# The order of the terms in a split matmul stream, factors made a stage sooner, and the decays of a gated linear attention made later

## The chip, the cores and the metric

One core of one Trainium2 chip. The metric is the device time of one execution in microseconds; smaller is better. The kernel was timed in 3 runs.

## What is computed

One layer of a streaming encoder for 512 tokens of width 2048, all in float32. The input projection of the normalised input is cut into nine parts: q, k, v and gate of a stick-breaking attention (8 heads of 128), q, k (512 wide), v and gate of a gated linear attention (4 heads), and a low-rank input of 16 columns for the decays.

```python
h = rms_norm(x, norm_gain[layer])
proj = jnp.einsum('bsd,de->bse', h, w_in[layer])
(sb_q, sb_k, sb_v, sb_g, gl_q, gl_k, gl_v, gl_g, gl_lr) = jnp.split(proj, offsets, axis=-1)
...
a_out = stick_breaking_attention(q, k, v)
a_out = from_heads(rms_norm(a_out, ...)) * jax.nn.silu(sb_g)
gate_logits = jnp.einsum('bsr,rk->bsk', gl_lr, gla_w_alpha[layer]) + gla_b_alpha[layer]
log_alpha = jax.nn.log_sigmoid(gate_logits.astype(jnp.float32)) / GLA_GATE_TAU
b_out = gated_linear_attention(..., log_alpha)
b_out = from_heads(rms_norm(b_out, ...)) * jax.nn.silu(gl_g)
mixed = jnp.concatenate([a_out, b_out], axis=-1)
x = x + jnp.einsum('bse,ed->bsd', mixed, w_out[layer])
```

The linear attention multiplies q by exp(cum) and k by exp(-cum), where cum is the running sum of log_alpha within a chunk: these are the decays of this text.

## The kernel before, in words

**Split products.** The large products run in a reduced float32 format (fp32r). To keep precision, each factor is held as two parts, hi (the rounded value) and lo (the rest), and a product is three terms: ah x hi, ah x lo and al x hi, where ah and al are the parts of the left factor (activations) and hi and lo those of the right one (weights). `split` (L173) makes a weight's parts: hi by a cast on ACT (L177), lo by a subtraction on DVE (L178), 128x1024 each. The parts of a left factor are made in `_split` (ACT L290, DVE L291, 128x512).

**Stages.** The work is ten stages in a row on TensorE (PE). Two are direct: q (tag q) and k (tag k), where `direct` (L293) sums over 4 units u and two parities odd, and for each of the two token halves issues 12 matmuls of 128x512 into two of the four accumulators z. The low-rank columns ride along in stage k (`rank_products`, L641, 4 matmuls after each half). The other eight are pairs (`pair`, L319): two 2048x512 weight blocks are done together by a scheme with 7 half-sized products in place of 8. Its left factors are blocks of the activations (A11, A12, A22) and sums of them: D = A22 - A21, NQ = -(D + A11), S3 = A11 - A21, S4 = D + A11 - A12. A pair goes through four sub-stages: (0, 1) A11 into x and D into y for each unit, (2) NQ into x and S4 into y, (3) A12 into y and S3 into x, then A22 into x; 28 products of 12 matmuls, which `mult` (L328) issues. The pairs are, in order: qv, vk, gqk (with the operands' roles exchanged, 24 matmuls of 128x256 a product), gv, ga, gb (all with the left factor h), then o0 and o1 (the output projection, left factor m, the gated mixture). In the names of tiles, hi_qva, qvp, qvq, qvb, qvc, qvd, qve are a pair's split weights in the order of use (a goes with A11, p with D, q with NQ, b with S4, c with A12, d with S3, e with A22); D_h, S_h, D_m, S_m are left factors, st and pw the weight tiles that `load` (L167) fetches and `add` (L183) sums, with `gather` (L188) adding a block by a DMA that GpSimd (POOL) issues.

**Left factors.** `Acts.get` gives a left factor for one unit. D and S3 are made at first use and kept; A11, A12, A22, NQ and S4 are written to DRAM and loaded again by each later pair. D costs a subtraction on DVE (L227) and a split, S3 the same (L216). h's D and S3 are first used in pair qv, m's in pair o0; m is complete for a group of columns when its two `gate` chains (L952) have run, counted in m_done.

**Order.** PE runs in the order of the program text. Everything that isn't a block product (the attention, the linear attention, the gates, the decays) is written as a generator; `side.step()`, which stands between block products, advances the first chain whose time has come. A chain yields a number, to be left alone for so many microseconds of matmul time as the program counts them, or a condition. The instructions of the other engines are put in order by a scheduler at build time, with a higher priority for what stands under `urgent()`; at run time each engine runs its own list. Side work takes one of four PSUM banks (`ptile`), block products four others: two accumulators x, two y. The next pair's x takes the banks that came free first, its y the last ones.

**Decays** (L667). After `low_rank` the chain waits 6.0, then for each of four heads issues one matmul (lg), copies it with its bias on ACT (lgs, L683, urgent), takes Abs, Exp and Ln on ACT (lge, L685 to L687), on DVE a combination (L688), a scan (L690) and a subtraction (L695), on ACT amid (L693) and two exponentials qe and ke (L697, L698), and on DVE three products with these (L701 to L704); it yields 3.0 between heads. The chain is spawned ahead of pair vk; gqk's results are multiplied by qe and ke, and wait for all four heads. The instructions of pair vk that end it are the evacuations of x_vk into sv_1 (ACT L153, DVE L157), scaled.

Of the kernel before, what the change touches and what calls it, by code (L numbers as in the profile page):

```python
# [13 lines left out]
P = 128  # L14
S = 512
D = 2048
NK = D // P
NB = S // P
KU = 2
NU = NK // KU  # L20
HU = NU // 2
H2 = 2 * P
# [71 lines left out]
def body(ctx: ExitStack, tc: tile.TileContext, x, xT, w_in, w_lr, w_alpha, vecs, w_out, out):  # L94
# [11 lines left out]
    side = Sides()  # L106

    def mm(o, l, r, **kw):
        n = r.free_size()
        side.t += n * (1.75 if l.dtype == F32 else 0.443) * 1e-3  # L110
        nc.tensor.matmul(o, l, r, **kw)  # L111
# [20 lines left out]
    def drop(n):  # L132
        held[0] -= n

    def room(n):
        return lambda: held[0] + n <= NU4
# [156 lines left out]
    def direct(A, s, tag, o, before=None, extra=None, last=False):  # L293

        z = [pacc.tile([P, S], F32, name=f"z_{tag}{j}", tag="acc") for j in range(NB)]
        for u in range(HU):
            for odd in range(2):
                if before is not None:
                    before(odd, u)
                hi, lo = split(load(s[odd * HU + u], f"{tag}{odd}{u}"), f"{tag}{odd}{u}")  # L300
                first, final = u == 0 and odd == 0, u == HU - 1 and odd == 1
                for half in range(2):
                    t = A.block(odd, half, u, last)
                    for a in range(2):
                        js = slice(a * P, (a + 1) * P)
                        for i in range(KU):
                            ah, al = t[:, 0, i, js], t[:, 1, i, js]
                            for n, (l, r) in enumerate(((ah, hi[:, i]), (ah, lo[:, i]), (al, hi[:, i]))):
                                mm(z[2 * half + a], l, r, start=first and i == 0 and n == 0,
                                   stop=final and i == KU - 1 and n == 2, skip_group_check=True)  # L310
                        side.step()
                    if extra is not None:
                        extra(odd, half, u, t)
        for half in range(2):
            o.finish(z[2 * half:2 * half + 2], half, 1.0, None)

# [2 lines left out]
    def pair(A, s1, s2, tag, o1, o2, order=(0, 1, 2, 3), tmajor=True, before=None):  # L319
# [3 lines left out]
        acc = {}  # L323
# [4 lines left out]
        def mult(f, u, w, acc, start, stop):  # L328
            t = A.get(f, u)
            hi, lo = w  # L330
            if tmajor:
                for a in range(2):
                    js = slice(a * P, (a + 1) * P)
                    for i in range(KU):
                        ah, al = t[:, 0, i, js], t[:, 1, i, js]
                        for n, (l, r) in enumerate(((ah, hi[:, i]), (ah, lo[:, i]), (al, hi[:, i]))):
                            mm(acc[a], l, r, start=start and i == 0 and n == 0,
                               stop=stop and i == KU - 1 and n == 2, skip_group_check=True)
                    if a == 0:
                        side.step()  # L340
            else:
                for c in range(4):
                    cs = slice(c * P, (c + 1) * P)
                    o = acc[c // 2][:, (c % 2) * H2:(c % 2 + 1) * H2]
                    for i in range(KU):
                        ah, al = t[:, 0, i], t[:, 1, i]
                        for n, (l, r) in enumerate(((hi[:, i, cs], ah), (hi[:, i, cs], al), (lo[:, i, cs], ah))):
                            mm(o, l, r, start=start and i == 0 and n == 0 and c % 2 == 0,
                               stop=stop and i == KU - 1 and n == 2, skip_group_check=True)
                    if c == 1:  # L350
                        side.step()
            side.step()

        first, last = order[0], order[-1]
# [191 lines left out]
    ps = ptile("warm_ps")  # L546
# [65 lines left out]
    lr = {}  # L612
# [25 lines left out]
        nc.vector.tensor_tensor(wa[64:96, :], wst[0:32, :], wa[0:32, :].bitcast(F32), ALU.subtract)  # L638
        low.append(wl)

    def rank_products(odd, half, u, t):  # L641

        if "ps" not in lr:
            lr["ps"] = ptile("lr_ps")
            lr["n"] = 0
        ts = slice(half * H2, (half + 1) * H2)
        for i in range(KU):
            for hl in range(2):
                lr["n"] += 1
                mm(lr["ps"][:, ts], lr[odd][:, u * KU + i, :], t[:, hl, i], start=lr["n"] == 1, stop=lr["n"] == 4 * NK,  # L650
                   skip_group_check=True)
        if lr["n"] == 4 * NK:
            drop(2)

# [11 lines left out]

    def decays():  # L667
        yield lambda: "lr" in done
        yield 6.0
        yield room(5)  # L670
        wa, lrT = low[0][:, 0, :], low[0][:, 1, :]
        blk = ut("blk")[:, 0, :]
# [5 lines left out]
        for h in range(GH):  # L678
            ps = ptile(f"lg{h}")
# [26 lines left out]
            if h == GH - 1:  # L706
                drop(2)
            if h < GH - 1:
                yield 3.0
        done.add("decays")  # L710


# [237 lines left out]
    me, mo, m_done = {}, {}, [0] * 4  # L950
# [41 lines left out]
    h = Acts("h", lambda u: he[u], lambda u: ho[u], ("D", "S3"))  # L992
# [31 lines left out]
    for hd in range(4):  # L1024
        side.spawn(gla_head(hd, ki, qd, gv, hd == 3))
    pair(h, w_in[6], w_in[7], "ga", gate(0), gate(1))
    pair(h, w_in[12], w_in[13], "gb", gate(2), gate(3))
    drop(8)


# [1 line left out]
        if stage == 0:  # L1032
            side.until(lambda: m_done[u] == 2)

    m = Acts("m", lambda u: me[u], lambda u: mo[u], ("D", "S3"))
    order = (0, 1, 3, 2)
    pair(m, w_out[0], w_out[1], "o0", Residual(0), Residual(1), order=order, before=ready)
    drop(10)
# [45 lines left out]
```

## Time and profile before

| | us |
|---|---|
| runs | 918.75, 916.96, 923.38 |
| median | 918.75 |
| the profiled execution | 924.25 |
| its span on the core | 922.4 |

The profile shows one execution: every instruction of the five engines (PE TensorE, PEld its weight loads, DVE VectorE, ACT ScalarE, POOL GpSimd), what ended an engine's idle time, and the clock that TensorE was granted, as a share of 2.4 GHz (0.50 is the lower of its two levels, 1.2 GHz). Over the whole span the mean granted clock was 0.957. The stages begin at about 8 (q), 64 (k), 116 (qv), 203 (vk), 332 (gqk), 444 (gv), 540 (ga), 642 (gb), 730 (o0) and 834 us (o1).

### The profile page before, as it was taken

The numbers are of one execution on the slowest core, as the hardware profiler recorded it, in microseconds if no ns is written. First come the engines' busy times: TensorE is split into PE (matmuls) and PEld (weight loads), VectorE is DVE, ScalarE is ACT, GpSimd is POOL, SyncE is SP. The second block draws the span as 40 slices with busy tenths as digits, with TensorE's granted clock in tenths as the row PEclk, the third lists the DMA queues.
The fourth block names the chain that finished last, engine by engine and source line by source line (L and its number), as shares of the span: only waits on it lengthen the run. The fifth ranks groups of instructions, "written<-read, shape, count | busy, mean of one in ns | idle before, by whom it ended". The sixth has DMA issues, their size and how long they took to land.

```text
span 922.4 us, 11401 instructions
## 1 busy us (share of the span) xinstructions
PE 841.4 (91%) x4082; PEld 700.2 (76%) x4082; DVE 667.1 (72%) x821; ACT 482.4 (52%) x822; POOL 75.0 (8%) x113
## 2 busy tenths in 40 slices
PE   8889999899779899899799899999998899779988
PEld 5678877678657699899687688878886777658766
DVE  4441699669886897788865676769856999777654
ACT  4464466466775656554564336456644845433331
POOL 1000000101111120220100100100001000000000
PEclk8999999999879899999899999999999999899999
DMA  8878326994447664776348973599579637999894
GB/s 316 285 263 287 134 92 243 322 346 160 160 129 218 199 207 158 241 228 240 132 145 281 316 282 101 174 327 344 195 248 298 238 118 262 291 340 344 277 337 126
DMA packets 62040, 216.97 MB, mean 235 GB/s; under 512 B 7040, under 2 KB 7168, under 8 KB 61984
## 3 DMA queue, kind: packets, MB, share of 16 engines
q1 hardware_dynamic: 54928, 195.26, 58.9%
q0 software_dynamic: 4608, 16.78, 10.1%
q10 hardware_dynamic: 2448, 4.21, 1.2%
q8 instruction: 32, 0.52, 0.2%
q14 instruction: 24, 0.20, 0.1%
HBM read 191.06 MB, written 25.17 MB: 234 GB/s over the span
## 4 chain that ended last, share of the span: by engine, by line
PE 49%; DVE 20%; DMA 17%; issue 8%; ACT 5%; POOL 1%; SPq 0%; DVEq 0%; ACTq 0%; POOLq 0%
PE x_o L111 5%; PE z_k L111 4%; PE x_ga L111 4%; PE x_gb L111 3%; PE x_gv L111 3%; PE y_o L111 3%; PE z_q L111 3%; PE y_gqk L111 3%; PE x_gqk L111 3%; PE y_gb L111 3%; PE y_ga L111 2%; PE x_vk L111 2%; PE y_gv L111 2%; DMA st_o0d<-in_w_out 2%; PE a L111 2%
## 5 line engine op out<-in xcount | busy, mean ns | idle before, releaser
L111 PE MATMUL z_q<-hi_q,A_h 128*128 128x512 f32 x128 | 44.1, 422 | 8.9 <-ACT A_h L290 4.9
L111 PE MATMUL z_k<-hi_k,A_h 128*128 128x512 f32 x128 | 42.3, 391 | 0.0
L111 PEld LDWEIGHTS z_q<-hi_q,A_h 128*128 128x128 f32 x128 | 25.9, 204 | 17.4 <-ACT A_h L290 6.2
L111 PEld LDWEIGHTS z_k<-hi_k,A_h 128*128 128x128 f32 x128 | 24.1, 188 | 4.7
L111 PE MATMUL z_q<-lo_q,A_h 128*128 128x512 f32 x64 | 26.8, 419 | 0.5 <-DVE lo_q L178 0.5
L178 DVE TENSOR_TENSOR lo_k<-st_k,hi_k 128x1024 fp32r<-128x1024 f32 x8 | 9.8, 1224 | 23.6 <-ACT hi_k L177 23.6
L111 PE MATMUL z_k<-lo_k,A_h 128*128 128x512 f32 x64 | 25.1, 392 | 0.0
L188 POOL DMA_DIRECT2D pw_o<-in_w_out x8 | 7.0, 870 | 183.2 <-DVE st_o1d L183 80.0
L178 DVE TENSOR_TENSOR lo_q<-st_q,hi_q 128x1024 fp32r<-128x1024 f32 x8 | 9.7, 1223 | 12.5 <-ACT hi_q L177 12.5
L188 POOL DMA_DIRECT2D pw_qv<-in_w_in x4 | 3.6, 906 | 175.9 <-DVE st_qvd L183 175.9
L111 PE MATMUL x_o<-hi_o0d,S_m 128*128 128x512 f32 x32 | 12.5, 454 | 5.3 <-DVE S_m L291 4.4
L111 PEld LDWEIGHTS z_q<-lo_q,A_h 128*128 128x128 f32 x64 | 13.0, 203 | 3.7 <-DVE lo_q L178 1.0
L111 PE MATMUL x_vk<-hi_vkd,S_h 128*128 128x512 f32 x32 | 12.3, 436 | 3.7 <-ACT hi_vkd L177 3.7
L177 ACT CAST hi_q<-st_q 128x1024 fp32r<-128x1024 f32 x8 | 8.3, 1048 | 11.7 <-PE z_q L111 11.7
L111 PE MATMUL y_o<-hi_o0p,D_m 128*128 128x512 f32 x32 | 11.7, 429 | 2.5 <-ACT D_m L290 1.5
L111 PE MATMUL x_o<-hi_o1d,S_m 128*128 128x512 f32 x32 | 11.8, 432 | 2.3 <-ACT hi_o1d L177 2.3
L943 ACT ACTIVATE ja<-an 128x128 f32<-128x128 f32 x32 | 9.9, 308 | 7.6 <-DVE an L155 7.0
L111 PE MATMUL x_qv<-hi_qvd,S_h 128*128 128x512 f32 x32 | 11.5, 423 | 2.5 <-ACT hi_qvd L177 2.5
L111 PEld LDWEIGHTS z_k<-lo_k,A_h 128*128 128x128 f32 x64 | 12.1, 189 | 1.9
L587 ACT ACTIVATE xt<-xt 128x1024 f32<-128x1024 f32 x8 | 8.5, 1061 | 9.6 <-DMA xt<-in_x 9.6
L111 PE MATMUL y_vk<-hi_vkb,S_h 128*128 128x512 f32 x32 | 13.4, 470 | 0.0
L860 ACT ACTIVATE cs_B<-cs_B 128x512 f32<-128x512 f32 x8 | 5.1, 633 | 16.0 <-POOL cs_B L858 15.8
(644 smaller groups left out, 2970.2 us busy)
## 6 DMA issues: line engine op xcount, KB each, us to landing
A_h<-far_A_h SPq DMA_DIRECT2D x72, 512.0 KB, 5.5
NQ_h<-far_NQ_h SPq DMA_DIRECT2D x20, 512.0 KB, 4.3
S_h<-far_S_h SPq DMA_DIRECT2D x20, 512.0 KB, 3.4
far_A_h<-A_h SPq DMA_DIRECT2D x12, 512.0 KB, 4.0
far_A_m<-A_m SPq DMA_DIRECT2D x12, 512.0 KB, 7.3
A_m<-far_A_m SPq DMA_DIRECT2D x12, 512.0 KB, 7.9
st_q<-in_w_in SPq DMA_DIRECT2D x8, 512.0 KB, 4.5
st_k<-in_w_in SPq DMA_DIRECT2D x8, 512.0 KB, 3.8
```

Of the source, the lines that this page charges most:

```text
L111: nc.tensor.matmul(o, l, r, **kw)
L177: nc.scalar.copy(hi, t)
L178: nc.vector.tensor_tensor(lo, t, hi.bitcast(F32), ALU.subtract)
L188: nc.gpsimd.dma_start(t, src, accum_op=ALU.add)
L587: nc.scalar.activation(xt, xt, AF.Square, accum_out=ss8[:, j * 2 + i:j * 2 + i + 1])
L860: nc.scalar.activation(cs, cs, AF.Exp)
L943: nc.scalar.activation(junk, an[:, tb * P:(tb + 1) * P], AF.Square, accum_out=ss[:, tb:tb + 1])
```

## The change

Four parts. (A) In `direct` and `mult` the terms with hi (8 of a product's 12 matmuls) come first for the whole product and the terms with lo last; `direct` takes both token halves together, 16 matmuls with hi and 8 with lo, and the low-rank matmuls of both halves come behind them. (B) `rank_products` makes D and S3 of h, unit by unit, during stage k. (C) The left factor m is declared ahead of pair gb, and in gb's sub-stages 2 and 3, at the units 1 and 3, D and S3 of m's groups 0 and 1 are made. (D) The decays' first wait is 50.0 instead of 6.0, and that between heads 8.0 instead of 3.0. In `mult` the branch with exchanged roles (gqk) is changed in the same way as the one shown.

```diff
                 first, final = u == 0 and odd == 0, u == HU - 1 and odd == 1
-                for half in range(2):
-                    t = A.block(odd, half, u, last)
-                    for a in range(2):
-                        js = slice(a * P, (a + 1) * P)
+                ts = [A.block(odd, half, u, last) for half in range(2)]
+                for low_part in (False, True):
+                    for j in range(NB):
+                        t, js = ts[j // 2], slice(j % 2 * P, (j % 2 + 1) * P)
                         for i in range(KU):
                             ah, al = t[:, 0, i, js], t[:, 1, i, js]
-                            for n, (l, r) in enumerate(((ah, hi[:, i]), (ah, lo[:, i]), (al, hi[:, i]))):
-                                mm(z[2 * half + a], l, r, start=first and i == 0 and n == 0,
-                                   stop=final and i == KU - 1 and n == 2, skip_group_check=True)
-                        side.step()
-                    if extra is not None:
-                        extra(odd, half, u, t)
+                            if low_part:
+                                mm(z[j], ah, lo[:, i], start=False, stop=final and i == KU - 1, skip_group_check=True)
+                            else:
+                                mm(z[j], ah, hi[:, i], start=first and i == 0, stop=False, skip_group_check=True)
+                                mm(z[j], al, hi[:, i], start=False, stop=False, skip_group_check=True)
+                        if j % 2:
+                            side.step()
+                if extra is not None:
+                    extra(odd, u, ts)
...
             if tmajor:
-                for a in range(2):
-                    js = slice(a * P, (a + 1) * P)
-                    for i in range(KU):
-                        ah, al = t[:, 0, i, js], t[:, 1, i, js]
-                        for n, (l, r) in enumerate(((ah, hi[:, i]), (ah, lo[:, i]), (al, hi[:, i]))):
-                            mm(acc[a], l, r, start=start and i == 0 and n == 0,
-                               stop=stop and i == KU - 1 and n == 2, skip_group_check=True)
-                    if a == 0:
+                for low_part in (False, True):
+                    for a in range(2):
+                        js = slice(a * P, (a + 1) * P)
+                        for i in range(KU):
+                            ah, al = t[:, 0, i, js], t[:, 1, i, js]
+                            if low_part:
+                                mm(acc[a], ah, lo[:, i], start=False, stop=stop and i == KU - 1, skip_group_check=True)
+                            else:
+                                mm(acc[a], ah, hi[:, i], start=start and i == 0, stop=False, skip_group_check=True)
+                                mm(acc[a], al, hi[:, i], start=False, stop=False, skip_group_check=True)
+                    if not low_part:
                         side.step()
...
-    def rank_products(odd, half, u, t):
+    def rank_products(odd, u, blocks):
...
+        if odd:
+            h.get("D", u)
+            h.get("S3", u)
         if lr["n"] == 4 * NK:
...
         yield lambda: "lr" in done
-        yield 6.0
+        yield 50.0
         yield room(5)
...
             if h < GH - 1:
-                yield 3.0
+                yield 8.0
...
-    pair(h, w_in[12], w_in[13], "gb", gate(2), gate(3))
+    m = Acts("m", lambda u: me[u], lambda u: mo[u], ("D", "S3"))
+
+    def ahead(stage, u):
+        if stage >= 2 and u in (1, 3):
+            n = stage - 2
+            side.until(lambda: m_done[n] == 2)
+            side.until(room(3))
+            m.get("D" if u == 1 else "S3", n)
+
+    pair(h, w_in[12], w_in[13], "gb", gate(2), gate(3), before=ahead)
...
-    m = Acts("m", lambda u: me[u], lambda u: mo[u], ("D", "S3"))
```

On PE, the last unit of pair qv's sub-stage 3 (x_qv_920 and 921, after the change 958 and 959, are the two accumulators x; hi_qvd and lo_qvd the split weights, S_h the left factor S3). Before:

```order
L111 MATMUL x_qv_920<-hi_qvd_1478,S_h_1483 128x512
L111 MATMUL x_qv_920<-lo_qvd_1479,S_h_1483 128x512
L111 MATMUL x_qv_920<-hi_qvd_1478,S_h_1483 128x512 x2
L111 MATMUL x_qv_920<-lo_qvd_1479,S_h_1483 128x512
L111 MATMUL x_qv_920<-hi_qvd_1478,S_h_1483 128x512
L111 MATMUL x_qv_921<-hi_qvd_1478,S_h_1483 128x512
```

After:

```order
L111 MATMUL x_qv_958<-hi_qvd_1483,S_h_914 128x512 x4
L111 MATMUL x_qv_959<-hi_qvd_1483,S_h_914 128x512 x4
L111 MATMUL x_qv_958<-lo_qvd_1484,S_h_914 128x512 x2
L111 MATMUL x_qv_959<-lo_qvd_1484,S_h_914 128x512 x2
L111 MATMUL y_qv_960<-hi_qvc_1478,A_h_1503 128x512 x4
L111 MATMUL y_qv_961<-hi_qvc_1478,A_h_1503 128x512 x4
```

The second matmul of a product read lo; now the ninth does, and the last two of each accumulator. Behind them the next product (y_qv) begins with its hi terms.

On ACT, where pair vk ends and gqk begins (sv_1 is the evacuation of x_vk; lgs, lge, amid, qe and ke are steps of the decays; cs_B, an, y_k belong to the attention). Before:

```order
L860 ACTIVATE cs_A_2578<-cs_A_2578 128x512
L177 CAST hi_gqka_2789<-st_gqka_2785 128x1024
L177 CAST hi_gqkp_2832<-pw_gqk_2787 128x1024
L153 ACTIVATE sv_1_2778<-x_vk_1631,rstd 128x512
L177 CAST hi_gqka_2864<-st_gqka_2860 128x1024
L860 ACTIVATE cs_B_2639<-cs_B_2639 128x512
L554 ACTIVATE y_k_2691<-v_k_2688 128x16
```

After:

```order
L702 ACTIVATE lge_2632<-lge_2632 128x512
L701 ACTIVATE lge_2725<-lge_2725 128x512
L151 COPY an_2789<-a_2777 128x512
L702 ACTIVATE lge_2725<-lge_2725 128x512
L875 ACTIVATE cs_B_2601<-cs_B_2601 128x512
L565 ACTIVATE y_k_2678<-v_k_2675 128x16
L708 ACTIVATE amid_2638<-lge_2632 128x4
L566 ACTIVATE y_k_2678<-y_k_2678 128x16
L712 ACTIVATE qe_2371<-lgs_2630 128x512
L713 ACTIVATE ke_2372<-lgs_2630 128x512
L153 ACTIVATE sv_1_2744<-x_vk_1630,rstd 128x512
```

Before, sv_1 came right after two casts of weights; now steps of the decays of two heads stand ahead of it, qe and ke among them.

On DVE, the same place (the other half of sv_1; w_A is the evacuation of the transposes wT_A of PE, lo_gqkp the lo of the weights for gqk's first y product). Before:

```order
L946 TENSOR_TENSOR on_1_2331<-an_2539,r_a_2557 128x2x128
L854 SCALAR_TENSOR_TENSOR cs_B_2639<-runs,e_B_2632 128x512
L178 TENSOR_TENSOR lo_gqkp_2833<-pw_gqk_2787,hi_gqkp_2832 128x1024
L157 TENSOR_SCALAR sv_1_2778<-x_vk_1630,rstd 128x512
L855 TENSOR_TENSOR cs_B_2639<-zB_2624,cs_B_2639 128x512
L808 TENSOR_TENSOR v_k_2688<-ss_k_1627,rstd_104 128x16
```

After:

```order
L178 TENSOR_TENSOR lo_gqkp_2896<-pw_gqk_2862,hi_gqkp_2895 128x1024
L155 COPY w_A_2568<-wT_A_2819 128x512
L183 TENSOR_TENSOR pw_gqk_2753<-pw_gqk_2753,st_gqkb_3123 128x1024
L870 TENSOR_TENSOR cs_B_2601<-zB_2586,cs_B_2601 128x512
L703 SCALAR_TENSOR_TENSOR lgs_2630<-lgs_2630,lge_2632 128x512
L824 TENSOR_SCALAR v_k_2675<-v_k_2675 128x16
L705 SCALAR_TENSOR_TENSOR lge_2632<-blk,lgs_2630 128x512
L703 SCALAR_TENSOR_TENSOR lgs_2723<-lgs_2723,lge_2725 128x512
L710 TENSOR_TENSOR lgs_2630<-lge_2632 128x512
L568 TENSOR_TENSOR t_k_2681<-y_k_2678 128x16
L705 SCALAR_TENSOR_TENSOR lge_2725<-blk,lgs_2723 128x512
L157 TENSOR_SCALAR sv_1_2744<-x_vk_1631,rstd 128x512
```

The evacuation sv_1 followed lo_gqkp; now it stands behind w_A, an addition of weights and the decays' combination, scan and subtraction.

On DVE in pair gb, sub-stage 3 (st_gbd is the weight sum for S3 of h, one per unit; lo_gbc and lo_gbd the lo parts; D_m and dq_m steps of D of m; ge and z steps of the gates). Before:

```order
L183 TENSOR_TENSOR st_gbd_6081<-pw_gb_5726,st_gbd_6081 128x1024
L958 TENSOR_SCALAR z_0_6029<-z_0_6029 128x1024
L178 TENSOR_TENSOR lo_gbc_6084<-st_gbc_6079,hi_gbc_6083 128x1024
L178 TENSOR_TENSOR lo_gbd_6089<-st_gbd_6081,hi_gbd_6088 128x1024
L178 TENSOR_TENSOR lo_gbc_6124<-st_gbc_6119,hi_gbc_6123 128x1024
L965 TENSOR_TENSOR ge_0_6055<-ge_0_6055,z_0_6029 128x1024
L183 TENSOR_TENSOR st_gbd_6121<-pw_gb_5771,st_gbd_6121 128x1024
L969 TENSOR_TENSOR ge_0_6055<-ge_0_6055,on_0_5199 128x1024
L178 TENSOR_TENSOR lo_gbd_6129<-st_gbd_6121,hi_gbd_6128 128x1024
```

After:

```order
L183 TENSOR_TENSOR st_gbd_6095<-pw_gb_5726,st_gbd_6095 128x1024
L291 TENSOR_TENSOR D_m_6089<-dq_m_5909,D_m_6089 128x512
L235 TENSOR_TENSOR dq_m_5909<-dq_m_5909,me_5499 128x512
L183 TENSOR_TENSOR st_gbd_6135<-pw_gb_5771,st_gbd_6135 128x1024
L178 TENSOR_TENSOR lo_gbd_6103<-st_gbd_6095,hi_gbd_6102 128x1024
L980 TENSOR_TENSOR ge_0_6067<-ge_0_6067,z_0_6039 128x1024
L178 TENSOR_TENSOR lo_gbc_6138<-st_gbc_6133,hi_gbc_6137 128x1024
L984 TENSOR_TENSOR ge_0_6067<-ge_0_6067,on_0_5199 128x1024
L178 TENSOR_TENSOR lo_gbd_6143<-st_gbd_6135,hi_gbd_6142 128x1024
```

The lo of the second unit (lo_gbd_6089, after the change lo_gbd_6103) came before the third unit's sum; now it comes behind it and behind two steps of D of m.

## Rows read from the trace of the kernel before

**Rows 1.** The page's first part: busy us, share of the span, instructions.

```profile
PE 841.4 (91%) x4082; PEld 700.2 (76%) x4082; DVE 667.1 (72%) x821; ACT 482.4 (52%) x822; POOL 75.0 (8%) x113
```

**Rows 2.** TensorE's waits: line, released by, us in total, times, longest.

```profile
PE T_q L115 <- ACT lgs L683: 6.9, 1, 6.9
...
PE x_o L111 <- DVE S_m L291: 4.4, 1, 4.4
...
PE x_o L111 <- DVE lo_o0e L178: 4.0, 1, 4.0
...
PE T_k L115 <- ACT lgs L683: 3.6, 1, 3.6
...
PE y_gqk L111 <- DVE lo_gqkb L178: 2.4, 1, 2.4
...
PE wT_C L115 <- DVE cs_A L855: 2.2, 1, 2.2
...
PE y_o L111 <- ACT D_m L290: 1.5, 1, 1.5
...
PE y_o L111 <- DVE D_m L291: 1.0, 1, 1.0
...
PE y_gb L111 <- DVE lo_gbb L178: 0.3, 1, 0.3
```

**Rows 3.** Windows: stretch, length, busy of PE, PEld, DVE, ACT, POOL; clock; DMA share, GB/s.

```profile
64.00:116.00 52.00, 52.00 (x260) 44.13 (x259) 21.08 (x34) 26.13 (x67) 0.00 (x0) 1.00 0.56 193
116.00:203.00 87.00, 80.46 (x345) 64.46 (x345) 74.14 (x91) 49.17 (x90) 4.26 (x6) 0.98 0.73 247
130.00:145.00 15.00, 12.53 (x57) 9.53 (x55) 14.21 (x23) 9.09 (x15) 0.00 (x0) 1.00 0.21 70
160.00:175.00 15.00, 14.39 (x64) 11.58 (x63) 12.47 (x16) 7.45 (x10) 1.88 (x2) 1.00 1.03 336
203.00:332.00 129.00, 110.16 (x516) 91.05 (x515) 105.18 (x136) 86.64 (x184) 24.17 (x34) 0.91 0.60 190
249.80:256.60 6.80, 5.41 (x15) 4.44 (x16) 6.73 (x11) 2.65 (x6) 1.56 (x3) 0.50 0.35 60
263.40:270.30 6.90, 4.69 (x15) 3.79 (x16) 6.80 (x11) 5.31 (x9) 0.92 (x2) 0.51 0.20 76
290.00:332.00 42.00, 35.92 (x172) 29.47 (x171) 34.72 (x48) 24.93 (x61) 11.88 (x14) 0.92 0.70 220
730.00:765.00 35.00, 30.06 (x123) 23.40 (x122) 33.97 (x44) 17.60 (x23) 0.00 (x0) 0.91 0.32 115
792.50:799.30 6.80, 5.08 (x12) 4.02 (x13) 5.74 (x7) 1.94 (x3) 0.86 (x1) 0.50 0.87 253
```

**Rows 4.** The chain that ended last: start us, us, what (pair gb; pair o0).

```profile
655.21 2.72 PE x_gb L111 x12
...
784.12 8.19 DMA st_o0d<-in_w_out
...
792.34 1.23 DVE st_o0d L183
793.56 0.60 DVE S_m L291
```

**Rows 5.** Timeline of DVE: start us, us, line, tiles, idle before and releaser.

```profile
245.31 0.68 DVE L688 SCALAR_TENSOR_TENSOR lgs<-lgs,lge 128x512 f32<-128x512 f32 x1
246.03 1.23 DVE L690 TENSOR_TENSOR_SCAN lge<-blk,lgs 128x512 f32<-128x512 f32 x1
...
330.79 0.74 DVE L157 TENSOR_SCALAR sv<-x_vk,rstd 128x512 f32<-128x512 f32 x1
...
703.34 1.22 DVE L183 TENSOR_TENSOR st_gbd<-pw_gb,st_gbd 128x1024 f32<-128x1024 f32 x1 [2.42 <-DMA st_gbd<-in_w_in]
```

**Rows 6.** Timeline of ACT, decays in vk and the end of vk.

```profile
262.68 0.63 ACT L697 ACTIVATE qe<-lgs 128x512 f32<-128x512 f32 x1 [0.97 <-DVE lgs L695]
...
329.67 0.69 ACT L153 ACTIVATE sv<-x_vk,rstd 128x512 f32<-128x512 f32 x1 [1.67 <-PE x_vk L111]
```

More of the change, by code (lines that the diff above doesn't have):

```diff
@@ L340, in mult @@
                         side.step()
             else:
[L342 to L350, printed above, removed]
+                for low_part in (False, True):
+                    for c in range(4):
+                        cs = slice(c * P, (c + 1) * P)
+                        o = acc[c // 2][:, (c % 2) * H2:(c % 2 + 1) * H2]
+                        for i in range(KU):
+                            ah, al = t[:, 0, i], t[:, 1, i]
+                            if low_part:
+                                mm(o, lo[:, i, cs], ah, start=False, stop=stop and i == KU - 1, skip_group_check=True)
+                            else:
+                                mm(o, hi[:, i, cs], ah, start=start and i == 0 and c % 2 == 0, stop=False,
+                                   skip_group_check=True)
+                                mm(o, hi[:, i, cs], al, start=False, stop=False, skip_group_check=True)
+                    if not low_part:
@@ L645, in rank_products @@
             lr["n"] = 0
[L646 to L651, printed above, removed]
+        for half, t in enumerate(blocks):
+            ts = slice(half * H2, (half + 1) * H2)
+            for i in range(KU):
+                for hl in range(2):
+                    lr["n"] += 1
+                    mm(lr["ps"][:, ts], lr[odd][:, u * KU + i, :], t[:, hl, i], start=lr["n"] == 1,
+                       stop=lr["n"] == 4 * NK, skip_group_check=True)
+        if odd:
+            h.get("D", u)
+            h.get("S3", u)
         if lr["n"] == 4 * NK:
```

## The prediction

> **What bounds the kernel now.** I read the busy time of the engines first, then TensorE's list of waits, then a table of windows by stage, then the chain of waits, and last the timelines of single stretches. The reader is to see in [rows 1] that TensorE (PE) is busy for 841.4 of 922.4 us: the bound is the matmul stream, and all that a change of order can win is the 81 us in which it stands and the time in which it runs at the lower of its two levels. The wait list [rows 2] names who makes it stand: casts and subtractions that split the weights, left factors made too late (D_m, S_m), and two transposes (T_q, T_k) that wait for the PSUM bank which `lgs`, the first step of the decays, has not yet emptied. The windows [rows 3] give the price that follows a stand: after the waits of the decays the granted clock is 0.50 and 0.51 (the 1.2 GHz level) for 6.8 and 6.9 us, after the wait for S_m 0.50 for 6.8 us. Half of the PE time in such a stretch is a loss: (5.41 + 4.69) / 2 = 5.0 us for the first two together. Undisturbed, a product of 12 matmuls takes 2.72 us [rows 4], 0.227 us a matmul.
>
> **A, hi terms first.** The matmuls stay the same in number and shape. Before, the first matmul that reads lo stood one behind the first that reads hi; now eight stand ahead of it (see the order of the pair qv). That is 7 x 0.227 = 1.59 us more for the subtraction on VectorE (DVE), which takes 1.2 us. TensorE's waits for a lo of L178 are 17 rows of the list, the first 4.0 and the last 0.3 us [rows 2], 20.2 us in sum. The two rows over 1.6 us (4.0 and 2.4) keep 2.4 and 0.8; the rest, 17.0 us, could go. That is the upper end. But DVE is what is late there: where it is behind by its own queue, the wait comes back a product later, at hi. The lower end is 0: the left factor's lo is read 0.23 us sooner than before, and the first of two banks is finished two matmuls from the end instead of six, so its evacuation starts 0.9 us later. I take 8, near the middle, as most rows are single waits of under 1.6 us with cover enough and a few are not.
>
> **B, D and S3 of h in the direct k stage.** Per unit: four DVE instructions of 128x512 (0.68 us by [rows 5]) and two casts on ScalarE (ACT). For four units 16 x 0.68 = 11 us of DVE leave pair qv. They issue no DMA, since these factors are kept. In qv, DVE is busy 74.14 of 87.00 us, and in 130 to 145 us 14.21 of 15.00 while PE has 12.53 [rows 3]. In the k stage PE never stands, and DVE is busy for 21.08 of 52.00: it hides the 11 us there. One lo_k can fall back by the 2.7 us of a unit's four; sixteen hi matmuls now stand ahead of its first reader, 15 x 0.227 = 3.4 us, and without that cover each unit would cost up to 2.7. The most that can be won is qv's idle time, 87.00 - 80.46 = 6.5, with the 2% that the clock lacks, 1.7: 8. The least is 0, if the loads end last there. I take 5, nearer the upper end as the engine full in that stretch is the one relieved.
>
> **C, D and S3 of m, groups 0 and 1, inside pair gb.** 8 DVE instructions (5.4 us) and 4 casts leave o0 and its first stretch, where DVE is busy 33.97 of 35.00 us [rows 3]. There y_o waits 1.5 and 1.0 us for D_m, and x_o 4.4 us for S_m [rows 2]; the half clock after the latter costs 5.08 / 2 = 2.5 [rows 3]. The sum, 9.4, and 2.6 for half of the first stretch's missing clock make the upper end, 12; the D_m waits alone, 2.5, make the lower. I take 6: S_m stands behind an addition (`st_o0d`, L183) that waits for a load of 8.19 us [rows 4], so part of it becomes a wait for that load's own split. The price is in gb. The order shows `lo_gbd_6103` (the lo of the second unit of that stage) now behind two D_m steps and behind the third unit's addition `st_gbd_6135`, which waits for its load: before, such an addition waited 2.42 and took 1.22 us [rows 5]. Less A's cover, 2.42 + 1.22 - 1.59 = 2; with D_m's two steps and a half clock 7. I take 2 lost (0 to 7).
>
> **D, the decays later and spread.** Removed from vk: T_q 6.9, T_k 3.6 and wT_C 2.2 [rows 2], with the 5.0 of half clock 17.7 us, the upper end. The lower is T_q with its stretch, 6.9 + 2.3 = 9. I take 14: the attention's own work still fills DVE there (105.18 of 129.00 us, [rows 3]). But the work is moved, not removed: the decays' heads 2 and 3 now fall on the end of vk, where DVE is already busy 34.72 of 42.00 us. The order shows the new wait. At the change from vk to gqk the evacuations of x_vk (`sv_1`) free the banks that y_gqk needs. Before, they came at 329.67 and 330.79 us, right after the last x_vk, and the list has no wait of y_gqk for them [rows 2, 5, 6]. Now the DVE one stands behind `w_A`, which waits for wT_A on PE, and wT_A is the last thing PE does ahead of y_gqk. After wT_A, DVE has to do five steps of 128x512 (0.68), one of 128x1024 (1.22), two scans (1.23) and `sv_1` itself (0.74): 3.4 + 1.2 + 2.5 + 0.7 = 7.8 us [rows 5]. The ACT one stands behind `qe` and `ke` (0.63 each, [rows 6]), which wait for the seventh of those DVE steps: 5.9 + 1.3 + 0.7 = 7.8 as well. PE has nothing to do meanwhile, since its order is fixed. A half clock follows, as after T_q (2.3), and DVE's backlog ahead of `w_A` I put at 1.4: 11.5 lost. The low bound is 3 (7.0 by the overlap of DVE's steps, less 4 that the loads and splits gain while PE stands), the high one 17 (a backlog twice that of one addition and 6.8 us at half clock).
>
> Here the Trainium skill bears on the sum. The page "TensorE: Matmul & The Clock Gate", section "Architectural detail: the array is 16x 32x32, not 1x 128x128", says that ACT and DVE work strictly in order, and only TensorE pulls weight loads ahead. By that rule `sv_1` cannot pass the decays and the term is 11.5; if it could, the term would be 0. The trace agrees: S_m stood behind an addition that waited for a load and came as soon as it was done [rows 4].
>
> **Sum**, against the profiled execution (924.25 us, span 922.4): -8 - 5 - 6 + 2 - 14 + 11.5 = -19.5, so 904.75. The profiled execution lies 5.5 above the median of the runs (918.75), so on the median's scale 899.25; I say 899.
>
> **Rivals.**
> R1, the new stand is given back. While PE waits at y_gqk, DVE, ACT and the loads run ahead, and the later waits of gqk (y_gqk for lo_gqkb, 2.4) and of gv shrink by as much. For it: all these waits are for splits and loads. Against it: gqk has few waits to give. All gains without the 11.5: 924.25 - 31 = 893.25, on the median's scale 888.
> R2, the DMA engines take over. In 160 to 175 us they are busy at a share of 1.03 and 336 GB/s [rows 3], and in o0 the chain of waits runs through a load of 8.19 us [rows 4]. If the stages with three loads a unit are bound by transfers, A, B and half of C turn into waits for st tiles: -3 + 2 - 14 + 11.5 = -3.5, so 920.75, and 915 on the median's scale: the same within what can be told. Against it: the wait list has no DMA as the last to come, and DVE is fuller.
> The Trainium skill ("Trainium Kernel Development and Optimization", section "Key Constraints") says that transfers issued from any queue run on the same 16 DMA engines and interleave. By that rule POOL's gathers lengthen the loads just there, which speaks for R2.
> R3, slower: the four `lg` banks. Each `lg` takes one of four side banks until ACT empties it; the attention's transposes queue for the same banks. In their new place, the last products of vk, where ACT also has the sv evacuations and `cs`, each could hold PE as T_q was held: 4 x (6.9 + 2.5) = 38 us, and 14 gained in the old place. Then -17 - 14 + 38 + 11.5 = +18.5: 942.75, on the median's scale 937. It decides from where the decays' new costs together exceed 31 us. For it: one bank did cost 6.9 us. Against it: `lgs` is urgent, and the four are now spread by 8 us and more of PE time.
>
> **Chances.** Forecast 50%, R1 20%, R2 18%, R3 12%. The forecast's own range: the half widths of the terms (A 8, B 4, C 5, gb 3, D 4 and its wait 7), added as squares, make 13, so 886 to 912. A measurement of this kernel can tell about 1% (9 us, below 909.6) from no change. R1 and 0.44 of the forecast's 0.50 are faster by that: 0.64; R2 and the rest of the forecast make same, 0.24; R3 makes slower, 0.12. The range leaves out R3 and some 8% at its two ends: 876 (R1 with A at its upper end and a little more) to 922 (R2 with gb at its upper end, 920, and 2 less from C).
>
> **What would show it.** Right: waits for lo in single places gone or under 0.8 us; none of T_q and T_k for lgs in vk; y_gqk's first matmul with 8 us or so idle ahead of it, released by `sv`, and a half clock behind; no waits for D_m or S_m of groups 0 and 1. Wrong: y_gqk without idle time (R1's side of D); waits for hi or for st loads in place of those for lo (R2); waits of several us for lgs in the last 40 us of vk (R3). A time above 928 would make the forecast wrong in sign, one below 876 in size.

## The result and the profile after

The changed kernel takes 918.35 us (median of 20 runs, 913.9 to 922.96) beside 923.4 us for the kernel before (20 runs, 916.8 to 928.6). The ratio is 0.9949 (0.9927 to 0.9971): 4.7 us or 0.5% faster, where 19.5 us were forecast, and too little for the bound of 1%. The profiled execution has a span of 918.9 us at a mean granted clock of 0.966.

The first part of the changed kernel's page, which answers to [rows 1]:

```profile
PE 829.1 (90%) x4082; PEld 692.7 (75%) x4082; DVE 665.4 (72%) x821; ACT 481.3 (52%) x822; POOL 68.4 (7%) x113
```

Busy time fell by 12 us and the span by 3.5 alone, so TensorE stands for longer than before: 918.9 - 829.1 = 90 us in place of 81. The matmuls are the same 4082, and the busy time fell because the granted clock rose from 0.957 to 0.966: 841.4 x 0.957 = 805 and 829.1 x 0.966 = 801 us at the full clock. The list of waits says where TensorE stands (columns as in [rows 2]):

```profile
PE y_o L111 <- DVE xr L512: 9.9, 1, 9.9
PE y_gqk L111 <- DVE sv L157: 8.4, 1, 8.4
PE x_gb L111 <- ACT hi_gbd L177: 8.3, 2, 6.2
PE wT_A L115 <- ACT lgs L698: 4.5, 1, 4.5
...
PE x_ga L111 <- DVE lo_gae L178: 1.3, 1, 1.3
...
PE y_o L111 <- DVE S_m L291: 1.0, 1, 1.0
...
PE y_o L111 <- DVE D_m L291: 1.0, 2, 0.8
...
PE y_gb L111 <- DVE lo_gbb L178: 0.5, 1, 0.5
```

The reader is to compare this with [rows 2]. Gone are T_q and T_k for lgs (10.5 us in sum); S_m's 4.4 are down to 1.0, D_m's 2.5 to 1.0, and of the waits for lo 4.4 us are left (5 rows, the first and last shown, in place of 17 rows with 20.2). New are four rows at the top: 9.9 for xr, 8.4 for sv, 8.3 for hi_gbd and 4.5 for lgs, 31 us together. One of them, sv, was in the prediction; the longest wasn't.

The windows of the changed kernel by stage (columns as in [rows 3]; pairs qv, vk, gqk, gb, o0, o1, and the stretch right behind the wait for sv):

```profile
112.90:200.70 87.80, 81.09 (x347) 65.72 (x345) 65.68 (x74) 46.51 (x92) 3.63 (x4) 0.96 0.73 247
200.70:305.40 104.70, 99.36 (x494) 82.99 (x493) 87.17 (x106) 72.01 (x144) 16.96 (x33) 0.98 0.65 215
305.40:438.00 132.60, 109.55 (x870) 106.91 (x868) 109.29 (x149) 80.10 (x159) 19.48 (x35) 0.94 0.58 191
631.80:728.10 96.30, 85.82 (x377) 69.34 (x376) 76.70 (x84) 53.38 (x66) 3.48 (x4) 0.95 0.76 252
728.10:820.70 92.60, 82.69 (x353) 65.91 (x352) 79.98 (x96) 45.82 (x59) 3.48 (x4) 0.96 0.77 266
820.70:914.60 93.90, 80.47 (x335) 65.57 (x336) 52.92 (x52) 26.22 (x25) 3.48 (x4) 0.93 0.78 257
326.10:330.00 3.90, 3.85 (x18) 3.86 (x19) 3.87 (x10) 2.97 (x13) 0.00 (x0) 0.50 0.02 4
```

Taken from one stage's first block matmul to the next one's (o1 to the start of its last matmul), in the timelines of one profiled execution each, the stages last (us):

| kernel | qv | vk | gqk | gv | ga | gb | o0 | o1 |
|---|---|---|---|---|---|---|---|---|
| before | 87.2 | 128.6 | 112.3 | 96.1 | 102.4 | 87.3 | 104.0 | 84.6 |
| after | 87.8 | 104.7 | 132.6 | 89.3 | 104.6 | 96.4 | 92.6 | 93.9 |
| e_noC | 82.3 | 104.8 | 133.1 | 89.8 | 104.6 | 91.0 | 100.0 | 80.7 |
| f_xrurgent | 83.0 | 103.7 | 132.7 | 89.6 | 104.9 | 94.7 | 92.9 | 82.6 |
| h_CD | 83.0 | 105.0 | 132.6 | 89.1 | 105.2 | 86.3 | 92.6 | 80.6 |
| h_CS3 | 82.6 | 103.8 | 132.8 | 90.5 | 104.3 | 90.6 | 99.0 | 95.3 |
| g_gap12 | 84.2 | 107.5 | 120.2 | 92.8 | 104.3 | 95.9 | 93.4 | 93.1 |
| h_gap12_CD | 83.1 | 111.7 | 117.9 | 93.1 | 104.1 | 89.7 | 95.1 | 78.9 |

So vk gave 24 us and gqk took 20 of them (some of it is work that moved: gqk has 870 matmuls in place of 851, vk 494 in place of 513); o0 gave 11, and gb and o1 took 18. Stage qv varies between 82 and 88 us from one execution to the next with the same code in it, and no reading rests on it.

**The wait for sv.** DVE's timeline at the change from vk to gqk, and below it PE's, the transposes wT_A and the first matmuls of y_gqk:

```profile
317.56 1.20 DVE L178 TENSOR_TENSOR lo_gqkp<-pw_gqk,hi_gqkp 128x1024 fp32r<-128x1024 f32 x1
318.68 0.68 DVE L155 COPY w_A<-wT_A 128x512 f32<-128x512 f32 x1
319.28 1.22 DVE L183 TENSOR_TENSOR pw_gqk<-pw_gqk,st_gqkb 128x1024 f32<-128x1024 f32 x1
320.41 0.69 DVE L870 TENSOR_TENSOR cs_B<-zB,cs_B 128x512 f32<-128x512 f32 x1
321.01 0.68 DVE L703 SCALAR_TENSOR_TENSOR lgs<-lgs,lge 128x512 f32<-128x512 f32 x1
...
321.79 1.21 DVE L705 TENSOR_TENSOR_SCAN lge<-blk,lgs 128x512 f32<-128x512 f32 x1
322.92 0.71 DVE L703 SCALAR_TENSOR_TENSOR lgs<-lgs,lge 128x512 f32<-128x512 f32 x1
323.55 0.68 DVE L710 TENSOR_TENSOR lgs<-lge 128x512 f32<-128x512 f32 x1
...
324.24 1.21 DVE L705 TENSOR_TENSOR_SCAN lge<-blk,lgs 128x512 f32<-128x512 f32 x1
325.37 0.72 DVE L157 TENSOR_SCALAR sv<-x_vk,rstd 128x512 f32<-128x512 f32 x1
```

```profile
316.85 0.87 PE L115 MATMUL wT_A<-ident,cs_A 128*128 128x128 f32 x4 [4.52 <-ACT lgs L698]
326.15 2.07 PE L111 MATMUL y_gqk<-D_h,hi_gqkp 128*128 128x256 f32 x8 [8.43 <-DVE sv L157]
```

The steps stand in the queue as the order showed them: `w_A` starts when wT_A is done, then an addition, `cs_B`, the decays of two heads, and sv last. From the start of `w_A` to the end of sv it is 7.4 us (7.8 were forecast); DVE is 1.0 us late for `w_A` (1.4 forecast). The first y_gqk begins 0.06 us after sv. The granted clock right behind is 0.50 for 3.9 us, with PE busy all the time: 1.9 us more.

**The wait for xr.** This is the last of o0 and the first of o1: SP's queue, DVE, then PE. y_gqk's pattern comes again here: o1's y products need the banks that o0's last x leaves, and xr, the residual's x, is loaded and then added to that x (L512), which empties the bank.

```profile
823.96 0.41 SPq L253 DMA_DIRECT2D NQ_m<-far_NQ_m  x1
824.85 14.21 SPq L494 DMA_DIRECT2D xr<-in_x  x8
```

```profile
821.70 0.68 DVE L512 TENSOR_TENSOR xr<-xr,x_o 128x512 f32<-128x512 f32 x1
...
831.93 1.22 DVE L183 TENSOR_TENSOR pw_o<-pw_o,st_o1b 128x1024 f32<-128x1024 f32 x1 [1.41 <-DMA st_o1b<-in_w_out]
833.83 0.69 DVE L512 TENSOR_TENSOR xr<-xr,x_o 128x512 f32<-128x512 f32 x1 [0.67 <-DMA xr<-in_x]
```

```profile
834.57 1.65 PE L111 MATMUL y_o<-hi_o1p,D_m 128*128 128x512 f32 x3 [9.92 <-DVE xr L512]
```

The first half was added at 821.70, the second at 833.83, 12 us later, when its load had come; y_o began behind that. In the kernel before both halves came in one go:

```profile
833.41 1.28 DVE L501 TENSOR_TENSOR xr<-xr,x_o 128x512 f32<-128x512 f32 x2
```

The second load was issued at 824.85, behind a reload of the left factor (NQ_m). Below are SP's instructions between the two loads of xr in program order, first before, then after the change (the names in full; xr0_2 and xr0_3 are the two halves):

```
before: xr0_2, st_o1a0, xr0_3
after:  xr0_2, st_o1a0, far_A12_m2, st_o1a1, far_A22_m0, far_A22_m1, far_A22_m3, pw_o10, pw_o11, far_A22_m2,
        A11_m0, A11_m1, pw_o13, st_o1a3, A11_m3, pw_o12, st_o1a2, A11_m2, st_o1b0, NQ_m0, xr0_3
```

Eighteen more instructions stand between them.

**The wait for hi_gbd.** The chain that ended last, in gb's sub-stage 3, when x_gb waited:

```profile
693.94 9.82 DMA st_gbc<-in_w_in
...
703.84 1.05 ACT hi_gbc L177
...
704.92 0.41 DVE lo_gbc L178
...
706.54 1.14 DVE st_gbd L183
```

It is a load of 9.82 us for st_gbc, with its cast, then the addition for st_gbd behind it on DVE. It is not lo_gbd, on which the prediction's price in gb rested.

### The profile page after: what moved, and what is told of

Read it like the earlier page. It is cut to its first block, busy times and chain, and to the rows that moved or that the text cites. A ratio compares the mean times of both kernels' runs of the same rounds, so it can differ in the third digit from the quotient of the medians.

```text
span 918.9 us, 11502 instructions
## 1 busy us (share of the span) xinstructions
PE 829.1 (90%) x4082; PEld 692.7 (75%) x4082; DVE 665.4 (72%) x821; ACT 481.3 (52%) x822; POOL 68.4 (7%) x113
## 4 chain that ended last, share of the span: by engine, by line
PE 24%; DMA 13%; DVE 9%; issue 3%; ACT 2%; DVEq 0%; SPq 0%; ACTq 0%
PE x_o L111 4%; PE x_gb L111 3%; PE y_o L111 3%; PE y_gv L111 3%; PE x_gv L111 2%; DMA st_gbc<-in_w_in 2%; PE x_ga L111 2%; PE y_gb L111 2%; PE y_ga L111 2%; DMA st_o1d<-in_w_out 2%; DMA st_gad<-in_w_in 1%; DMA pw_o<-in_w_out 1%; DMA st_o0c<-in_w_out 1%; PE o L111 1%; DMA xr<-in_x 1%
## 5 line engine op out<-in xcount | busy, mean ns | idle before, releaser
L111 PE MATMUL z_q<-hi_q,A_h 128*128 128x512 f32 x128 | 35.5, 431 | 6.8 <-DVE A_h L291 3.3
L111 PEld LDWEIGHTS z_q<-hi_q,A_h 128*128 128x128 f32 x128 | 26.5, 210 | 15.4 <-DVE A_h L291 4.2
L111 PE MATMUL z_k<-hi_k,A_h 128*128 128x512 f32 x128 | 30.6, 391 | 0.0
L111 PE MATMUL x_gb<-hi_gbd,S_h 128*128 128x512 f32 x32 | 10.8, 493 | 8.3 <-ACT hi_gbd L177 8.3
L111 PE MATMUL y_o<-hi_o1p,D_m 128*128 128x512 f32 x32 | 9.1, 424 | 9.9 <-DVE xr L512 9.9
L111 PE MATMUL y_gqk<-D_h,hi_gqkp 128*128 128x256 f32 x64 | 10.0, 319 | 8.4 <-DVE sv L157 8.4
L111 PEld LDWEIGHTS y_gqk<-D_h,hi_gqkp 128*128 128x128 f32 x64 | 9.5, 226 | 8.8 <-DVE sv L157 8.8
L111 PE MATMUL z_q<-lo_q,A_h 128*128 128x512 f32 x64 | 15.8, 389 | 0.0
L111 PE MATMUL z_k<-lo_k,A_h 128*128 128x512 f32 x64 | 15.8, 389 | 0.0
L111 PEld LDWEIGHTS x_gb<-hi_gbd,S_h 128*128 128x128 f32 x32 | 7.4, 237 | 10.8 <-ACT hi_gbd L177 9.2
L111 PEld LDWEIGHTS y_o<-hi_o1p,D_m 128*128 128x128 f32 x32 | 6.4, 204 | 11.6 <-DVE xr L512 10.3
```

## The experiments

Ratios are to the kernel before, run in the same jobs, with 95% intervals; 0.01 is 9.2 us.

**Taking one part away.** The first four kernels are the changed one, less one of its four parts.

`e_noA`, the terms interleaved again:

```diff
-                for low_part in (False, True):
...
+                        for n, (l, r) in enumerate(((ah, hi[:, i]), (ah, lo[:, i]), (al, hi[:, i]))):
```

> The changed kernel with the three terms of a product interleaved again (hi, lo, hi as before); B, C and D stay. If the hi terms first are worth what stage q and pair gv show (3 and 7 us less lost), the time is 10 us over the changed kernel: ratio to the kernel before 1.006, and the waits for lo come back to about 20 us. If the waits for lo only turn into waits for hi and for loads, it is 3 us over the changed kernel (q alone): ratio 0.998.

Measured: 1.0038 (1.0018 to 1.0059), 8 us over the changed kernel. TensorE's waits for lo come back as 20 rows with 31 us, of which the first and the last are below, behind the first part of the page:

```profile
PE 838.0 (91%) x4082; PEld 696.2 (75%) x4082; DVE 666.4 (72%) x821; ACT 482.6 (52%) x822; POOL 74.2 (8%) x113
...
PE x_vk L111 <- DVE lo_vkd L178: 4.2, 2, 3.0
...
PE x_o L111 <- DVE lo_o0q L178: 0.3, 1, 0.3
```

TensorE does not stand longer for it: 924.9 - 838.0 = 87 us beside 90 in the changed kernel. What is lost stands in the busy time, at a mean granted clock of 0.961 in place of 0.966.

`e_noB`, without the two lines in `rank_products`:

```diff
-        if odd:
-            h.get("D", u)
-            h.get("S3", u)
```

> The changed kernel with D and S3 of h made in pair qv again. If qv ends on its loads (it lost 10.0 us before and 10.6 after), B is worth nothing: ratio 0.995, the same as the changed kernel. By the prediction, B is worth 5 us: ratio 1.000.

Measured: 0.9975 (0.9948 to 1.0001): 2.4 us over the changed kernel, which can't tell 5 from 0.

`e_noC`, without the early D and S3 of m:

```diff
-    pair(h, w_in[12], w_in[13], "gb", gate(2), gate(3), before=ahead)
+    pair(h, w_in[12], w_in[13], "gb", gate(2), gate(3))
```

> The changed kernel without the early D and S3 of m. Theory: the late load of xr (9.9 us at o1's start) and the 8.3 us of hi_gbd in gb come with C; both go, and o0 loses some 11 again: 7 us under the changed kernel, ratio 0.987. Rival: these two waits come from PE arriving earlier at its loads, whatever C does; they stay, and o0 loses 11 more: ratio 1.007.

Measured: 0.9852 (0.9812 to 0.9891), 9 us under the changed kernel. The wait for xr is gone, o1 lasts 80.7 us in place of 93.9, gb 91.0 in place of 96.4, and o0 is 7 us longer. The rival falls.

`e_noD`, the decays' waits at 6.0 and 3.0 again:

```diff
-        yield 50.0
+        yield 6.0
...
-                yield 8.0
+                yield 3.0
```

> The changed kernel with the decays' waits at 6.0 and 3.0 again. Theory: y_gqk's wait for sv (8.4 us) goes and T_q's and T_k's waits for lgs come back: vk loses some 22 more and gqk 17 less, so 5 us over the changed kernel, ratio 1.000. Rival: vk's gain came from A and B rather than D; then only gqk's 17 go and the ratio is 0.977.

Measured: 1.0010 (0.9983 to 1.0036), 5.6 us over the changed kernel, as the theory has it. The waits of vk are back:

```profile
PE T_q L115 <- ACT lgs L698: 5.3, 1, 5.3
...
PE T_k L115 <- ACT lgs L698: 4.8, 1, 4.8
PE wT_C L115 <- DVE cs_A L870: 4.7, 1, 4.7
```

**One part alone** on the kernel before. `e_onlyA`:

> The kernel before with the hi terms first alone. By the prediction's term of 8 us: ratio 0.991. If only waits of q and gv go (10 us): 0.989. If waits for lo turn into waits for hi: 0.997 or more.

Measured: 0.9943 (0.9921 to 0.9965), a gain of 5 us. The first part of its page:

```profile
PE 833.2 (91%) x4082; PEld 694.6 (76%) x4082; DVE 664.6 (73%) x821; ACT 481.6 (53%) x822; POOL 67.9 (7%) x113
```

The waits for lo fell from 20.2 to 5.9 us, but TensorE's waits of all kinds sum to 77.9 us, beside 77.1 in the kernel before. In these two executions the whole gain stands in the busy time, 8.2 us less at a mean granted clock of 0.966 in place of 0.957; over all runs of the two kernels here the mean clocks are 0.967 and 0.963, which by the 805 us at full clock (805 / 0.963 - 805 / 0.967) is 3 of the 5 us.

`e_onlyC`:

> The kernel before with the early D and S3 of m alone. Theory (C moves the load of xr behind other loads and fills gb): o0 gains some 11 us, gb and o1 lose some 18: 7 us over the kernel before, ratio 1.008, with y_o waiting about 10 us for xr. By the prediction's terms (6 gained, 2 lost): ratio 0.996.

Measured: 1.0040 (1.0017 to 1.0062), a loss of 4 us, with y_o waiting 8.1 us for xr. C is a loss by itself.

`e_onlyD`:

> The kernel before with the later decays alone. The order has the same decays steps ahead of sv_1 as in the changed kernel. Theory: vk gains 22 and gqk loses 17: ratio 0.995. By the prediction's terms (14 gained, 11.5 lost): 0.997. Rival: without A, vk keeps its waits for other things and D is a loss: 1.005 or more.

Measured: 0.9960 (0.9936 to 0.9984), a gain of 4 us. y_gqk stands for 9.1 us here too, put down to `amid` of the decays on ACT.

**The two waits by themselves.** `f_xrurgent` is the changed kernel with one line at high priority:

```diff
         def _x(self, half, a):
...
-            nc.sync.dma_start(t, x[j * P:(j + 1) * P, self.g * S:(self.g + 1) * S])
+            with urgent():
+                nc.sync.dma_start(t, x[j * P:(j + 1) * P, self.g * S:(self.g + 1) * S])
```

> The changed kernel with the loads of xr (the residual's x) issued at high priority, which puts the second one of o0's end right behind the first on SP's queue. Theory: the 9.9 us of y_o at o1's start go: ratio 0.985 with the half clock that followed. Rival: the load of xr only covered a wait for the weights of o1, which is late anyway; then most of the 9.9 comes back as waits for hi_o1p or st_o1a: 0.993 or more.

Measured: 0.9846 (0.9817 to 0.9875), 9.5 us under the changed kernel. DVE's timeline has both halves together again:

```profile
815.22 1.28 DVE L513 TENSOR_TENSOR xr<-xr,x_o 128x512 f32<-128x512 f32 x2
```

`g_gap12` is the changed kernel with another number:

```diff
             if h < GH - 1:
-                yield 8.0
+                yield 12.0
```

> The changed kernel with 12.0 instead of 8.0 between the decays' heads; nothing else. In the order, sv_1 then stands behind lo_gqkp with no decays step ahead, and the last two heads fall into gqk. Theory (the 8.4 us of y_gqk for sv and the half clock behind it are the price of the decays' steps ahead of sv_1): y_gqk no longer waits for sv, gqk loses some 10 less, ratio 0.984. Rival R1 (what PE stands there is given back later anyway): the ratio stays at 0.995, other waits of gqk grow.

Measured: 0.9840 (0.9806 to 0.9874), 10 us under the changed kernel. On DVE sv starts 1.8 us after lo_gqkp, and y_gqk comes with no wait behind wT_A:

```profile
303.84 1.21 DVE L178 TENSOR_TENSOR lo_gqkp<-pw_gqk,hi_gqkp 128x1024 fp32r<-128x1024 f32 x1
...
305.64 0.74 DVE L157 TENSOR_SCALAR sv<-x_vk,rstd 128x512 f32<-128x512 f32 x1
```

```profile
307.18 0.60 PE L115 MATMUL wT_A<-ident,cs_A 128*128 128x128 f32 x4
307.54 2.16 PE L111 MATMUL y_gqk<-D_h,hi_gqkp 128*128 128x256 f32 x16
```

The edit took away two waits and not one: that of wT_A for lgs (4.5 us) is gone from the list as well. With the half clock behind sv (1.9) it is 14.8 us at the place, of which 10 are left at the end; gqk is 12 us shorter, vk and gv 3 each longer. So most of what TensorE stood there was not given back later, and rival R1 falls; but the 10 us are the price of both waits, and no run takes sv's away alone.

`g_gap12_xr`, both edits together:

> The changed kernel with both repairs: 12.0 between the heads and the loads of xr at high priority. If the two prices are independent (10 us each): ratio 0.974. If the second only shifts what the first leaves: 0.982 or more.

Measured: 0.9737 (0.9704 to 0.9771). The two gains add up, 10 and 9.5 us, and 20 together, within an interval of some 3 us each.

`g_gap12_noC`, 12.0 and no C:

> The changed kernel with 12.0 between the heads and without the early D and S3 of m. If C without its late load of xr is worth what o0 gains (7 to 11) less what gb loses (4 to 5): 4 us slower than with both repairs, ratio 0.978. If C is worth nothing even so: 0.974, the same as with both repairs.

Measured: 0.9717 (0.9678 to 0.9756), the same as with both edits within the interval. With xr repaired, C is worth nothing as a whole.

`g_28_8_xr`, xr at high priority and the first wait of the decays at 28.0:

> The changed kernel with the loads of xr at high priority and the decays' first wait at 28.0 instead of 50.0 (8.0 between heads stays). No decays step stands ahead of sv_1, but the four heads fall into the middle of vk. If only the place of sv_1 counts: 0.974 as with 12.0. If the middle of vk charges for the decays as before (T_q and T_k wait for lgs): 0.984 or more.

Measured: 0.9781 (0.9747 to 0.9816), 6 us under f_xrurgent, with vk at 123.0 us and gqk at 108.2. In its list y_gqk has no wait for sv, and wT_A none for lgs. The place of the decays at the end of vk counts, and the middle of vk charges for the decays too, though at other instructions than before:

```profile
PE x_vk L111 <- ACT ke L714: 9.3, 1, 9.3
...
PE x_vk L111 <- DVE n_k L445: 6.9, 1, 6.9
```

**The halves of C.** The two kernels below keep one half each of what `ahead` makes. The expectations name one group, but both kernels make their half for the groups 0 and 1, as the changed kernel does.

```diff
-        if stage >= 2 and u in (1, 3):
+        if stage >= 2 and u == 1:
...
-            m.get("D" if u == 1 else "S3", n)
+            m.get("D", n)
```

> The changed kernel with only D of m's group 0 made early in gb (S3 and group 1's share left to o0). In the order, the loads of xr stand where they stood before. Theory (the early S3, which takes one of the seven buffers that xr also uses, moves xr, and the price of C is xr): the 9.9 us go, ratio 0.985 as without C. Rival (any early step of m in gb moves the rest): 0.990 or more.

Measured: 0.9697 (0.9669 to 0.9725). That is 23 us under the changed kernel and 14 under no C at all, where 9 and nothing were expected: the early D gains by itself, with what `ahead` does for it. `ahead` first runs the gates' chains to their end (`side.until`), and the waits of their transposes for the gates (mT for ge), 4.8 us in e_noC, are 0.8 us here; no run tells this apart from the early D. Of the list of waits:

```profile
PE y_gqk L111 <- DVE sv L157: 8.2, 1, 8.2
...
PE x_o L111 <- DVE S_m L291: 2.7, 3, 1.6
...
PE x_gb L111 <- ACT hi_gbd L177: 0.6, 1, 0.6
```

hi_gbd's 8.3 us are down to 0.6, and gb lasts 86.3 us.

`h_CS3`, with `u == 3` and `m.get("S3", n)`:

> The changed kernel with only S3 of m's group 1 made early (no early D). In the order, the second xr of o0's end is as late as in the changed kernel. Theory: the price of xr stays, 8 to 10 us of y_o: ratio 0.995. Rival (D in gb is what costs): 0.985.

Measured: 0.9996 (0.9975 to 1.0018), 13 us over no C. Of the list of waits:

```profile
PE y_o L111 <- DVE xr L512: 10.3, 1, 10.3
...
PE y_o L111 <- ACT D_m L290: 3.8, 1, 3.8
PE x_o L111 <- ACT hi_o0d L177: 3.7, 2, 2.4
```

The wait for xr is here. o0 lasts 99.0 us, as without C: an early S3 saves it next to nothing, since D_m is as late as before and x_o now waits for the weights' hi_o0d, which comes behind a load, in place of S_m.

`h_gap12_CD`, 12.0 and D alone:

> 12.0 between the heads, and only D of m's group 0 early. If an early D is worth the D_m waits of o0 (1.5 and 1.0 us in the kernel before): 0.969 against 0.9717 without C. If gb loses as much: 0.972.

Measured: 0.9643 (0.9610 to 0.9675), 890.5 us: 33 us under the kernel before, and the fastest of all. It is 7 us under `g_gap12_noC`, more than the 2.5 expected.

`h_gap12_noCB`, 12.0, neither C nor B:

> 12.0 between the heads, without C and with D and S3 of h made in pair qv again: B taken from the best version. By the prediction's term B is worth 5 us: ratio 0.977. If qv ends on its loads, B is worth nothing: 0.972.

Measured: 0.9759 (0.9724 to 0.9794), 3.9 us over `g_gap12_noC`.

## Why the prediction was wrong

It was wrong in size: 2.1% faster was forecast and 0.5% measured, because the price of C was looked for on one queue and stood on another. The 899 us were also counted from a median of three runs (918.75); twenty runs have it at 923.4, from which the sum gives 904. That the measured 918.35 lies between 876 and 922 is luck: that end of the range was there for R2. Two bounds were summed wrongly, without moving the forecast: half of the first stretch's missing clock is 35 x 0.09 / 2 = 1.6 and not 2.6 (C), and 6.8 us at the half clock cost 3.4 and not 6.8 (sv). Point by point:

- A (8 us, bounds 0 to 17): right in size, which is in part luck. It is 5 us alone, 8 in the company of the rest. The term priced the waits for lo and gave the clock nothing. The waits for lo did go (20.2 to 5.9 us alone), but other waits grew by as much, and in the profiled executions the gain is busy time at a higher granted clock (`e_onlyA`, `e_noA`). Why the clock rose with this order is not shown.
- B (5 us, 0 to 8): not settled. The two comparisons give 2.4 and 3.9 us, neither clear of the uncertainty of both kernels it compares, and qv itself scatters by 6 us.
- D: right in its net size, and in the place, the queue and the row of the wait for sv. Gain and price net at -2.5 us by the prediction, -4 to -6 measured. The price of sv was forecast at 11.5; at the place it is 8.4 of wait and 1.9 of half clock, 10.3. What it is worth at the end was measured only together with the wait for lgs (g_gap12: 10 for both). The gain in vk was larger than 14 (the stage is 24 us shorter), and gqk took 20, some of it for the wait of 4.5 us for lgs, which is R3's mechanism at one of four places.
- C (6 gained, 2 lost): this is the step that failed, in its price of 2 us (0 to 7). Measured, C costs 4 us alone and 9 in the changed kernel; by stage (e_noC beside the changed kernel) it gains 7 in o0 and loses 5 in gb and 13 in o1. The gain was there: o0 is 11 us shorter than before, 7 of it by the early D (e_noC against h_CD; the rest is A's and the run's scatter). The price was looked for on one queue, DVE in gb, where lo_gbd now stood behind the third unit's addition; that wait did not come. The prediction left out SP's queue. There the loads of xr went behind the weights and left factors of the next pair, which cost 9.5 us at the start of o1 (f_xrurgent), and four of them fell into gb's sub-stages 2 and 3, at 670 to 707 us, where they had been issued between 597 and 617 before. The halves tell whose it is: with D alone the loads stand where they stood, with S3 alone they don't. S3 takes a buffer of the kind that xr and the sums of S3 share; that this is how the scheduler comes to put xr later is read from the orders and was not tried by itself. Where gb's 8.3 us for hi_gbd come from stays open. Xr's four loads in gb do not make them by themselves: e_onlyC, e_noA and h_CS3 have such loads there (from 660 to 702 us) with no wait for hi_gbd, and gb at 86.3, 87.5 and 90.6 us. The wait of 6 to 8 us came in every kernel that has A, the early D and the early S3 together (f_xrurgent and g_gap12_xr too); no other has more than 0.6 us of it.
- R2 was not what cost the time at xr: that load was late by its place in a queue, and moving xr's loads ahead gave the time back. Its sign came in part: waits for hi rose from 15.6 to 26.5 us, 8.3 of them for hi_gbd, and three rows released by a DMA, 4.5 us, are new. R1, that all is given back, fell with g_gap12. R3's price for four banks came at one, 4.5 us.

The sum with what the runs showed: A -8, B -3, C +9, D with sv -5.6, together -7.6, beside the measured -4.7 (-6.7 to -2.7), each part taken from the changed kernel. The parts do not quite add up, and the interval of a part is some 3 to 4 us.

One size stays open: the early D gained 14 us without the repaired decays (h_CD against e_noC) and 7 with them (h_gap12_CD against g_gap12_noC). Each has an interval of 4 to 5 us. The profiles have o0 7 us shorter in both, and differ in gb and vk.

## What to carry to other kernels

A step that is made earlier can move loads on a queue where nothing of the step itself stands; here the moved loads share a pool of buffers with it. So compare all queues of the two programs for the whole program, the DMA queue first, and look at each last evacuation, since whatever stands ahead of it holds the next stage's accumulators. A move that costs may have one half that gains: here the early S3 had to go and the early D to stay, and with 12.0 between the heads that version is 3.6% faster than the kernel before. The work ahead of an evacuation could be summed here from the durations of its queue (7.8 us forecast, 7.4 measured); such a price is only as good as the list of the queues that were looked at.

## What the runs showed of the hardware

The wait for sv (8.4 us) was followed by 3.9 us at a granted clock of 0.50, as the waits of the kernel before were. Taking away a wait gave back about its own length for xr (9.9 us of wait, 9.5 at the end) and less for sv and lgs together (14.8 at the place with the half clock, 10 at the end).

The order of a product's terms showed in the granted clock: with the same matmuls and about the same sum of waits, TensorE was busy for 833.2 us at 0.966 with the hi terms first alone, and for 841.4 us at 0.957 before.
